# Accumulating DMAs in pieces of 8192 bytes, and a planner that runs GpSimd's and SyncE's transfers side by side

## The chip, the cores and the metric

The kernel runs on one core of one Trainium2 chip. The metric is the device time of one execution in microseconds (us). The engines are called TensorE (PE, with its weight loads PEld), VectorE (DVE), ScalarE (ACT), GpSimd (POOL) and SyncE (SP); each takes its instructions in order from a queue of its own. SyncE and GpSimd also issue DMAs, which run on the core's 16 DMA engines.

## The reference

One layer of a decoder trunk over 512 tokens of width 1024. A normed input is projected by one wide matrix; its columns feed four branches (forgetting attention A, an RG-LRU recurrence B, native sparse attention C, a spatial-gating MLP D). Each branch is gated and projected to 1024, the four are merged with sigmoid gates, and a last projection is added to the input.

```python
xn = rms_norm(x, norm_g)
z = xn @ w_in                      # 1024 x 10528
...
ys = jnp.stack([y_a * silu(ga), y_b * silu(gb), y_c * silu(gc), y_d * silu(gd)], axis=2)
proj = jnp.einsum('bsnw,nwd->bsnd', ys, w_branch)
merged = jnp.sum(jax.nn.sigmoid(mg.reshape(B, S, N_BRANCHES, D)) * proj, axis=2)
return x + merged @ w_out
```

All of it is float32.

## The kernel before

**Arithmetic.** Every float32 operand is split in a high part (a cast to fp32r) and a low part (the difference), and a product takes three matmuls of 128x512: high by high, low by high, high by low. For each weight tile of 128x1024 SyncE loads the raw 512 KB (`load`, tiles `r_...`, four buffers), GpSimd or ScalarE makes the high part (`hi_cast`), VectorE the low part (two subtractions, `wsplit`), and TensorE multiplies.

**Block sums.** The late projections (the gates mg0 to mg3, the branch projections wb1 and wb3, the output projection wo) are done with Strassen's scheme in Winograd's form: seven block products instead of eight, on sums and differences of weight blocks and of input blocks. The weight sums are formed in HBM by DMA alone: `sum_steps` lists for each family four base copies (`base`: s1, s3 from the weights, s2 from s1, 22 from s2) and four accumulating DMAs (`more`), which GpSimd issues and which add a block of 128 x 2048 floats (1 MB; for wb 128 x 1024 floats, 512 KB) to the copy in HBM. `x_sums` does the same with four sums of input blocks of 512 KB. A copy waits for the add whose result it reads, and an add for its base copy. The last argument of an accumulating DMA, `max_dma_last_dim`, is the largest piece in bytes in which a row is moved. The copies of mg0, mg2, mg1, wb1 and wb3 are issued by SyncE, those of mg3 and wo by GpSimd.

**Two ways of ordering.** Up to about 384 us (instructions that the profile puts on L231) all work is recorded first and then ordered by a planner, `Order`. From then on (L243) instructions stand in the order of the program text. The planner keeps a clock for each engine and a model of the shared things. `cost` gives each instruction a time to issue, a transfer time and, for DMAs, a delay until the data count as landed. `plan` then goes on engine by engine: whoever is free first takes, of the instructions whose needs are done at that time, the one that stands first in the program. The result is only an order for each engine's queue; at run time semaphores hold what isn't ready. So a cost in the planner moves no work by itself, but decides what stands behind what on each queue.

In the planner before, all DMAs share one wire: a transfer begins when the wire is free, at the earliest 1.3 us after its issue begins, takes size / 350e3 us from SyncE (size / 185e3 from GpSimd), and counts as done 0.86 us after its end; GpSimd's adds, and SyncE's DMAs into HBM tiles, count as done 10 us later still.

**Pace.** `tick` counts the steps of the dense matmul streams; every few steps (`BEAT`: 5 for the sums of this stretch) it records the next step of the sums, tied to the matmul just recorded. GpSimd's adds are moreover kept apart in the plan: each waits, in the plan alone, for the one before the last (`adds[-2]`).

**What GpSimd does besides.** In the planned stretch it makes most of the high parts of the weights, scales rows of the attention probabilities (p_a, p_s, p_w), fills operand tiles (`k_tiles` memsets kb_...; `spread` trs), copies key halves (`k_operand`, ka_...). After 384 us ScalarE takes over the casts of the block products, and GpSimd only paces (`paced_late`, tiles `mark`) and issues the late sums of mg3 and wo. The kernel is built with `dynamic_dma_scratch_size=1024`.

Of the kernel before, what the change touches and what calls it, by code (L numbers as in the profile page):

```python
# [14 lines left out]
ALU = mybir.AluOpType  # L15
AX = mybir.AxisListType
PSUM = bass.MemoryType.PSUM
# [50 lines left out]
class Order:  # L68
# [5 lines left out]
    def __init__(self, nc):  # L74
        self.eng = {"ACT": nc.scalar, "DVE": nc.vector, "POOL": nc.gpsimd, "PE": nc.tensor, "SP": nc.sync}
        self.on, self.ops, self.seen, self.ring, self.before, self.stacks = False, [], {}, {}, {}, {}
        self.free = dict.fromkeys(self.eng, 0.0)
        self.wire, self.shared, self.load, self.psum, self.bank = 0.0, (0.0, None), 0.0, set(), {}
        self.outside, self.floor, self.adds = set(), None, []
        self.end, self.pending, self.queued = {}, [], None  # L80

    def pool(self, real, stack, space):
# [48 lines left out]
    def cost(self, name, method, kw, aps):  # L131

        free = max(a.free_size() for _, a in aps)
        scalar = any(not w and x.free_size() == 1 for w, x in aps)
        wide = [x for w, x in aps if not w and x.free_size() > 1]
        if name == "PE":
            weights = kw["lhsT"] if "lhsT" in kw else wide[0]
            return aps[0][1].free_size() / 2400, 0.112 * max(64, min(128, weights.free_size())) / 128
        if method == "dma_start":
            size = 4  # L140
            for _, c in aps[0][1].ap:
                size *= c
            if name == "POOL":
                return 0.92, size / 185e3, 10.0
            return 0.37, size / 350e3, 10.0 if aps[0][1].tensor.name in self.outside else 0.0
        if name == "DVE":
            alone = bool(wide) and method not in ("tensor_reduce", "reciprocal", "memset") and not any(
                x.tensor.name in self.psum for x in wide)
            return 0.155 + free / 960 + 0.05 * scalar + 0.06 * (method == "tensor_tensor_scan" and free / 100), alone
        if name == "ACT":  # L150
            return 0.15 + free / 1140 + 0.09 * scalar + 0.15 * ("accum_out" in kw), False
        if method == "memset":
            return 0.1 + free / 1200, False
        return (0.09 + free / 540 if len(wide) > 1 and method == "tensor_tensor" else 0.18 + free / 1170), True
# [3 lines left out]
    def plan(self):  # L158

        ops, left, then, ready = self.ops, {}, {}, {}  # L160
        soon, able = {e: [] for e in self.eng}, {e: [] for e in self.eng}
        free, end, out = dict(self.free), self.end, []
        wire, shared, load, bank = self.wire, self.shared, self.load, dict(self.bank)
        margin = lambda e, m: self.WAKE[e] + (self.MARGIN[e] if ops[m][0] != e and ops[m][1] != "dma_start" else 0.0)
        for i in self.pending:
            name, need = ops[i][0], ops[i][4]
            for t in ops[i][6]:
                need.update((m, True) for m, *_ in self.seen.get(self.before.get(t), ()))
            ready[i], left[i] = 0.0, 0
            for m, whole in need.items():  # L170
                if m in end:
                    ready[i] = max(ready[i], end[m] + margin(name, m) if whole else 0.0)
                else:
                    left[i] += 1
                    then.setdefault(m, []).append(i)
            if not left[i]:
                heapq.heappush(soon[name], (ready[i], i))
        done, todo = {}, len(self.pending)
        while len(out) < todo:
            best = None  # L180
            for e in self.eng:
                t = free[e]
                while soon[e] and soon[e][0][0] <= t:
                    heapq.heappush(able[e], heapq.heappop(soon[e])[1])
                c = (t, e) if able[e] else (soon[e][0][0], e) if soon[e] else None
                best = min(best, c) if best and c else best or c
            t, e = best
            while soon[e] and soon[e][0][0] <= t:
                heapq.heappush(able[e], heapq.heappop(soon[e])[1])
            i = heapq.heappop(able[e])  # L190
            open_ = max((bank[x][1] + self.WAKE[e] for x in ops[i][7] if x in bank and bank[x][0] != e), default=0.0)
            if open_ > t:
                heapq.heappush(soon[e], (open_, i))
                continue
            a, b, *late = ops[i][5]
            if e == "PE":
                start = max(t + b, load)
                load, free[e], done[i] = start + a + 0.014, start + max(a - 0.098, 0.003), start + a + 0.172
            elif ops[i][1] == "dma_start":
                wire = max(wire, t + 1.3) + b  # L200
                free[e], done[i] = t + a, wire + 0.86 + sum(late)
            else:
                done[i] = t + a
                if b:
                    if shared[1] != e and shared[0] > t + 0.06:
                        done[i] = shared[0] - 0.06 + a
                    shared = done[i], e
                free[e] = done[i] - self.OVER[e]
            for x in ops[i][7]:
                bank[x] = e, done[i]  # L210
            out.append((i, dict(free), wire, shared, load, done[i]))
            for j in then.get(i, ()):
                f = ops[j][0]
                ready[j] = max(ready[j], done[i] + margin(f, i) if ops[j][4][i] else t)
                left[j] -= 1
                if not left[j]:
                    heapq.heappush(soon[f], (ready[j], j))
        return out
# [28 lines left out]
class _Pool:  # L247
    def __init__(self, order, real, space):
        self.order, self.real, self.names, self.lines = order, real, [], {}
        self.kind = {PSUM: order.psum, bass.MemoryType.DRAM: order.outside}.get(space, set())  # L250

    def tile(self, *args, tag=None, bufs=None, **kw):
        if tag is not None:
# [13 lines left out]
def tile_hybrid_layer(ctx: ExitStack, tc: tile.TileContext, x, xT, units, small, bsp, out):  # L267
    nc = tc.nc
    order = Order(nc)
    ACT, DVE, POOL, PE, DMA = (_Engine(order, e) for e in ("ACT", "DVE", "POOL", "PE", "SP"))  # L270
# [136 lines left out]
    def block(f, r, c):  # L407
        if f.startswith("wb"):
            return units[UIDX[f"{f}{c - 1}"], :, (r - 1) * 1024:r * 1024]
        return units[UIDX[f"{f}{c - 1}.{r - 1}"]]  # L410
# [3 lines left out]
    def sum_steps(f, copy):  # L414
        size = 1024 if f.startswith("wb") else 2048
        d = dsum[f] = {nm: dr.tile([P, size], F32, name=f"d{f}{nm}") for nm in ("s1", "s2", "22", "s3")}

        def base(nm, src):
            return lambda: copy.dma_start(d[nm], src)

        def more(nm, r, c):
            return lambda: POOL.dma_start(d[nm], block(f, r, c), accum_op=ALU.add, max_dma_last_dim=4096)

        return [base("s1", block(f, 1, 2)), base("s3", block(f, 1, 2)), more("s1", 1, 1), more("s3", 2, 2),
                base("s2", d["s1"]), more("s2", 2, 2), base("22", d["s2"]), more("22", 2, 1)]
# [180 lines left out]
    dxs = {nm: dr.tile([P, 1024], F32, name="dx" + nm) for nm in ("s1", "s2", "s3", "s4", "n11", "n21", "n22")}  # L606
# [8 lines left out]

    def x_sums():
        def more(nm, by):
            return lambda: POOL.dma_start(dxs[nm], dxs[by], accum_op=ALU.add, max_dma_last_dim=4096)

        return [more("s1", "n22"), more("s3", "n21"), lambda: DMA.dma_start(dxs["s2"], dxs["s1"]), more("s2", "n11"),  # L620
                more("s4", "s2")]
# [771 lines left out]
    late = ExitStack()  # L1393
# [535 lines left out]
```

## Time and profile before

| | |
|---|---|
| median of 3 runs | 703.0 us (702.05 to 704.62) |
| profiled execution | 705.58 us |
| its span, first to last instruction | 703.9 us |
| mean granted TensorE clock | 0.994 |
| DMA packets of SyncE's queue (q1) | 30208, 108.67 MB, 43.7% of 16 engines |
| DMA packets of GpSimd's queue (q0) | 7424, 35.65 MB, 24.7% of 16 engines |

A row of a group or of a timeline names the engine, the line of the code (a helper's line for nearly all instructions: L231 in the planned stretch, L243 behind it), the operation, and the tile written and those read; so instructions are found by their tiles. `dmg0s<-in_units_dram` is an add or a base copy for the sums of mg0, `dmg<-...` one for its tile 22, and `dwb1s`, `dmg3s`, `dwos`, `dxs` those of the others; POOLq marks a DMA that GpSimd issues, SPq one of SyncE. In a timeline what stands in brackets is how long the engine was idle before the row, and who ended that. A row of waits gives the engine and the tile that waited, who released it, and the us in total, the times and the longest. Durations of matmuls are longer than their share of the time, since matmuls overlap.

### The profile page before, as it was taken

What the parts mean: (1) busy time and instruction counts of PE and PEld (TensorE: products, weight loads), DVE (VectorE), ACT (ScalarE), POOL (GpSimd) and SP (SyncE); (2) the same over time, 40 slices, a digit from 0 to 9 for tenths busy, and PEclk for the clock granted to TensorE, in tenths of its full rate; (3) what the DMA queues carried; (4) which work ended last, traced back from release to release, by engine and by line L of the source; (5) the groups of instructions that cost most, each with busy time, mean ns of one, the idle gap of its engine ahead of it and who ended that gap; (6) DMA issues with size and microseconds to landing.
All of it is one profiled execution on the core that took longest, in us unless ns stands there. A gap on an engine that the chain in (4) does not pass through costs nothing.

```text
span 703.9 us, 9767 instructions
## 1 busy us (share of the span) xinstructions
PE 686.8 (98%) x3277; PEld 564.6 (80%) x3277; DVE 555.4 (79%) x1100; ACT 406.2 (58%) x766; POOL 202.5 (29%) x279
## 2 busy tenths in 40 slices
PE   8999999998979999999999999999999999999997
PEld 6888788887858888888777878888888888888886
DVE  6789778687576549898998669976888797948995
ACT  4563558575153127677656794445666666664861
POOL 4124864556173134445433122200110410100000
PEclk9999999999989999999999999999999999999999
DMA  8637078589789896976542224549899999997422
GB/s 312 247 119 240 25 215 270 152 203 247 162 248 311 223 237 192 202 153 185 106 87 78 88 85 155 168 142 383 250 313 310 301 328 327 314 307 259 142 90 90
DMA packets 38115, 145.44 MB, mean 207 GB/s; under 512 B 4129, under 2 KB 7585, under 8 KB 37665
## 3 DMA queue, kind: packets, MB, share of 16 engines
q1 hardware_dynamic: 30208, 108.67, 43.7%
q0 software_dynamic: 7424, 35.65, 24.7%
q8 instruction: 26, 0.43, 0.2%
q10 hardware_dynamic: 432, 0.49, 0.2%
q14 instruction: 25, 0.20, 0.1%
HBM read 139.56 MB, written 58.20 MB: 281 GB/s over the span
## 4 chain that ended last, share of the span: by engine, by line
PE 77%; DVE 9%; ACT 5%; issue 4%; POOL 2%; DMA 2%; SPq 0%; DVEq 0%; POOLq 0%; ACTq 0%
PE pj L243 4%; PE z_qc L231 3%; PE z_gd L231 3%; PE z_gb L243 3%; PE z_qa L231 3%; PE z_va L231 3%; PE tb L231 3%; PE z_ga L231 3%; PE outy L243 2%; PE mg0y L243 2%; PE mg3y L243 2%; PE mg1y L243 2%; PE mg2y L243 2%; PE z_ka L231 2%; PE o_s L231 2%
## 5 line engine op out<-in xcount | busy, mean ns | idle before, releaser
L243 DVE TENSOR_TENSOR w_mg<-r_mg,w_mg 128x512 fp32r<-128x512 f32 x48 | 31.9, 688 | 11.2 <-ACT w_mg L243 11.0
L243 PE MATMUL pj<-w_wb,yh 128*128 128x512 f32 x128 | 40.4, 390 | 0.0
L243 ACT CAST w_mg<-r_mg 128x1024 fp32r<-128x1024 f32 x24 | 25.2, 1049 | 10.3 <-issue 4.9
L243 POOL TENSOR_SCALAR mark<-mark 128x1 f32<-128x1 f32 x16 | 11.4, 711 | 66.6 <-ACT mark L243 66.5
L231 POOL TENSOR_SCALAR p_w<-p_w,nm_w 128x128 f32<-128x128 f32 (+3 forms) x32 | 18.1, 582 | 35.6 <-DVE nm_w L231 21.6
L243 PEld LDWEIGHTS pj<-w_wb,yh 128*128 128x128 f32 x128 | 24.0, 188 | 4.9
L231 POOL TENSOR_SCALAR p_s<-p_s,nm_s 128x128 f32<-128x128 f32 (+3 forms) x32 | 17.9, 593 | 28.3 <-DVE nm_s L231 19.4
L243 PE MATMUL pj<-w_wb,yl 128*128 128x512 f32 x64 | 25.4, 397 | 0.6 <-DVE yl L243 0.5
L231 ACT ACTIVATE p_w<-p_w,nm_w 128x256 f32<-128x256 f32 (+3 forms) x32 | 17.8, 555 | 13.9 <-DVE nm_w L231 12.3
L231 ACT CAST ph_a<-tb 128x512 fp32r<-128x512 f32 (+1 forms) x24 | 12.4, 518 | 20.2 <-PE tb L231 18.0
L231 PE MATMUL z_ga<-xh,w_ga 128*128 128x512 f32 x64 | 23.6, 426 | 0.4 <-DVE w_ga L231 0.4
L231 PE MATMUL z_xb<-xh,w_xb 128*128 128x512 f32 x64 | 23.2, 405 | 0.0
L231 PE MATMUL z_ud<-xh,w_ud 128*128 128x512 f32 x64 | 23.1, 411 | 0.0
L231 PE MATMUL z_gd<-xh,w_gd 128*128 128x512 f32 x64 | 22.7, 396 | 0.3 <-DVE sgd L231 0.3
L231 ACT ACTIVATE p_s<-p_s,nm_s 128x512 f32<-128x512 f32 (+3 forms) x32 | 17.9, 560 | 8.8 <-DVE nm_s L231 8.6
L231 ACT ACTIVATE p_a<-p_a,nm_a 128x512 f32<-128x512 f32 (+3 forms) x32 | 17.8, 558 | 8.2 <-DVE nm_a L231 8.1
L231 POOL TENSOR_SCALAR p_a<-p_a,nm_a 128x128 f32<-128x128 f32 (+3 forms) x32 | 18.6, 596 | 11.9 <-DVE nm_a L231 11.8
L243 DVE TENSOR_TENSOR w_wb<-r_wb,w_wb 128x512 fp32r<-128x512 f32 x28 | 18.3, 681 | 4.4 <-POOL w_wb L243 3.9
L243 PE MATMUL z_gb<-xh,w_gb 128*128 128x512 f32 x64 | 20.9, 390 | 0.0
L231 DVE CUSTOM_DVE_ANT_0 p_a<-s_a,maskm 128x512 f32<-128x512 f32 (+3 forms) x32 | 15.0, 486 | 5.6 <-PE tb L231 2.5
L231 DVE TENSOR_TENSOR pl_a<-tb,ph_a 128x512 fp32r<-128x512 f32 (+1 forms) x24 | 14.4, 598 | 4.7 <-ACT ph_a L231 4.5
L243 POOL TENSOR_SCALAR w_wb<-r_wb 128x1024 fp32r<-128x1024 f32 x8 | 10.1, 1264 | 26.9 <-PE pj L243 13.9
(744 smaller groups left out, 2419.4 us busy)
## 6 DMA issues: line engine op xcount, KB each, us to landing
r_mg<-in_units_dram SPq DMA_DIRECT2D x16, 512.0 KB, 6.9
r_wb<-in_units_dram SPq DMA_DIRECT2D x12, 512.0 KB, 5.0
dmg<-in_units_dram POOLq DMA_DIRECT2D x4, 1024.0 KB, 11.3
r_mg<-dmg SPq DMA_DIRECT2D x8, 512.0 KB, 9.0
dmg0s<-in_units_dram POOLq DMA_DIRECT2D x3, 1024.0 KB, 11.6
dmg2s<-in_units_dram POOLq DMA_DIRECT2D x3, 1024.0 KB, 11.3
dmg1s<-in_units_dram POOLq DMA_DIRECT2D x3, 1024.0 KB, 11.5
r_mg0s<-dmg0s SPq DMA_DIRECT2D x6, 512.0 KB, 4.7
```

Source lines behind the costliest of these rows:

```text
L231: getattr(self.eng[name], method)(*args, **kw)
L243: return lambda *args, **kw: real(*args, **kw).ins
```

## The change

Two things are changed. The accumulating DMAs of `sum_steps` and `x_sums` are cut in pieces of at most 8192 bytes instead of 4096. And the planner models two lanes of transfers: SyncE's, and GpSimd's adds. An add begins 1.7 us after its issue begins (or when the add before it is through), takes size / 155e3 us and 0.3 of the time it shares with a transfer of SyncE's, and counts as done 2.2 + 5 us later. A transfer of SyncE's runs at 0.33 of its rate while an add is on the way. Copies from HBM to HBM take size / 233e3 us, and what goes to an HBM tile counts as done 3 us later instead of 10. A new set `inner` holds the names of the SBUF tiles, by which the planner tells a copy from a store.

```diff
-        self.wire, self.shared, self.load, self.psum, self.bank = 0.0, (0.0, None), 0.0, set(), {}
-        self.outside, self.floor, self.adds = set(), None, []
+        self.wire, self.shared, self.load, self.psum, self.bank = (0.0, 0.0), (0.0, None), 0.0, set(), {}
+        self.inner, self.outside, self.floor, self.adds = set(), set(), None, []
...
             if name == "POOL":
-                return 0.92, size / 185e3, 10.0
-            return 0.37, size / 350e3, 10.0 if aps[0][1].tensor.name in self.outside else 0.0
+                return 0.92, size / 155e3, 5.0
+            inside, known = (aps[j][1].tensor.name in self.outside for j in (0, 1)), aps[1][1].tensor.name in self.inner
+            copy, source = inside
+            if copy and (source or not known):
+                return 0.37, size / 233e3, 3.0
+            return 0.37, size / 350e3, 3.0 if copy else 0.0
...
-        wire, shared, load, bank = self.wire, self.shared, self.load, dict(self.bank)
+        wire, added, shared, load, bank = *self.wire, self.shared, self.load, dict(self.bank)
...
             elif ops[i][1] == "dma_start":
-                wire = max(wire, t + 1.3) + b
-                free[e], done[i] = t + a, wire + 0.86 + sum(late)
+                free[e] = t + a
+                if e == "POOL":
+                    start = max(t + 1.7, added)
+                    added = start + b + 0.3 * min(b, max(0.0, wire - start))
+                    done[i] = added + 2.2 + late[0]
+                else:
+                    start = max(t + 1.3, wire)
+                    held = 0.33 * max(0.0, added - start)
+                    wire = start + b / 0.33 if held >= b else max(start, added) + b - held
+                    done[i] = wire + 0.86 + late[0]
...
-            out.append((i, dict(free), wire, shared, load, done[i]))
+            out.append((i, dict(free), (wire, added), shared, load, done[i]))
...
-        self.kind = {PSUM: order.psum, bass.MemoryType.DRAM: order.outside}.get(space, set())
+        self.kind = {PSUM: order.psum, bass.MemoryType.DRAM: order.outside}.get(space, order.inner)
...
-            return lambda: POOL.dma_start(d[nm], block(f, r, c), accum_op=ALU.add, max_dma_last_dim=4096)
+            return lambda: POOL.dma_start(d[nm], block(f, r, c), accum_op=ALU.add, max_dma_last_dim=8192)
...
-            return lambda: POOL.dma_start(dxs[nm], dxs[by], accum_op=ALU.add, max_dma_last_dim=4096)
+            return lambda: POOL.dma_start(dxs[nm], dxs[by], accum_op=ALU.add, max_dma_last_dim=8192)
```

## The prediction

> **What bounds the kernel now.** I read the page's busy shares first, then what TensorE (PE) waited for between 60 and 384 us, where the order is the planner's (ten rows, longest first; the six left out are at most 0.5 us each), then one row per stretch.
>
> ```profile
> span 703.9 us, 9767 instructions
> PE 686.8 (98%) x3277; PEld 564.6 (80%) x3277; DVE 555.4 (79%) x1100; ACT 406.2 (58%) x766; POOL 202.5 (29%) x279
> ```
> ```profile
> PE s_s L231 <- DVE q_c L231: 4.1, 1, 4.1
> PE o_a L231 <- DVE pl_a L231: 1.8, 1, 1.8
> PE s_w L231 <- DVE q_c L231: 1.2, 1, 1.2
> PE tb L231 <- DVE sc L231: 0.5, 1, 0.5
> ```
> ```profile
> core 0: us, PE busy (x) PEld busy (x) DVE busy (x) ACT busy (x) POOL busy (x), PEclk, DMA share, GB/s
> 158.00:174.00 16.00, 14.20 (x75) 11.20 (x74) 12.60 (x19) 8.06 (x19) 10.80 (x14) 1.00 0.98 282
> ...
> 199.50:204.00 4.50, 0.40 (x2) 0.01 (x1) 4.42 (x6) 2.74 (x4) 4.34 (x4) 1.00 0.94 192
> 204.00:212.00 8.00, 7.54 (x21) 5.36 (x22) 7.97 (x11) 2.41 (x3) 3.57 (x5) 0.57 0.75 175
> ...
> 440.00:640.00 200.00, 200.00 (x906) 166.44 (x905) 159.82 (x262) 118.89 (x168) 24.79 (x31) 1.00 0.89 289
> ```
>
> PE is the bound: 98% busy. So the change can win only what PE loses, and its largest loss is one place: 4.1 us without work near 200 us, and right behind it a granted clock of 0.57 over 8 us, which costs 8 x (1 - 0.57) = 3.4 us more. Together 7.5 us. The 1.8 us wait (it lies in 158 to 174) left the clock at 1.00. From 440 to 640 us PE is busy for all 200 us: nothing can be won there.
>
> Who made PE wait? The chain of waits from 174 to 205 us says it (a merged row's first number is its start, the second its length):
>
> ```profile
> 175.34 1.05 POOL w_vd.11_966 L231
> 176.38 9.26 issue
> ...
> 186.26 1.37 POOL w_ga L231
> 187.63 6.73 issue
> 194.36 0.91 POOL dmg2s L231
> ...
> 197.56 0.52 POOL kb_c L231
> ...
> 200.34 1.34 DVE trs L231
> ...
> 203.13 0.76 DVE q_c L231
> 203.88 0.14 issue
> 204.02 0.78 PE s_s L231 x2
> ```
>
> GpSimd (POOL) stood still twice, 9.26 + 6.73 = 16.0 us, each time just ahead of an accumulating DMA. Behind it on its in-order queue stood the cast of w_ga, the memsets of kb_c and of trs; VectorE waited for these, and PE for VectorE's q_c. "issue" means that no semaphore in the profile explains the stand. GpSimd's own timeline, and the landing of each of its DMAs (view of DMA issues, cut to the 1 us around each issue; last number is us from issue to landing), do:
>
> ```profile
> 174.05 0.93 POOL L231 DMA_DIRECT2D dmg2s<-in_units_dram  x1 [2.68 <-PE tb L231]
> 185.66 0.89 POOL L231 DMA_DIRECT2D dmg0s<-in_units_dram  x1 [9.28 <-issue]
> 194.36 0.91 POOL L231 DMA_DIRECT2D dmg2s<-in_units_dram  x1 [6.73 <-issue]
> 254.59 0.87 POOL L231 DMA_DIRECT2D dmg1s<-in_units_dram  x1
> 263.96 0.83 POOL L231 DMA_DIRECT2D dwb3s<-in_units_dram  x1
> ```
> ```profile
> dmg2s<-in_units_dram POOLq DMA_DIRECT2D x1, 1024.0 KB, 11.3
> ...
> dmg0s<-in_units_dram POOLq DMA_DIRECT2D x1, 1024.0 KB, 8.4
> ...
> dmg1s<-in_units_dram POOLq DMA_DIRECT2D x1, 1024.0 KB, 12.4
> ```
>
> 174.05 + 11.3 = 185.35, and the next add goes at 185.66. 185.66 + 8.4 = 194.06, and the next goes at 194.36. Twice an add of 1 MB is let go 0.3 us after the one before it has landed. But the 512 KB add of 263.96 went while the 1 MB add of 254.59 was still under way (254.59 + 12.4 = 267.0). A 1 MB add is 128 rows of 8192 bytes, now cut in 256 pieces; a 512 KB add has 128 pieces of 4096. So 256 + 128 pieces fit into whatever GpSimd's queue has room for, and 256 + 256 don't.
>
> **The change, part by part.**
>
> *Pieces of 8192 bytes.* A 1 MB add becomes 128 pieces; a 512 KB add keeps its 128, for its rows are 4096 bytes. 128 + 128 is less than the 256 + 128 that fit, and a third still fits. What goes is the stand ahead of the adds. What is late next at 200 us? ScalarE's q_c:
>
> ```profile
> 199.24 1.38 ACT L231 ACTIVATE q_c<-qt_c,cc 64x512 fp32r<-64x512 f32 x2 [0.44 <-PE qt_c L231]
> ```
>
> It ends at 200.62; VectorE's last q_c step (0.76) would then end near 201.4, and PE go on near 201.5 instead of 204.0. So at least 2.5 us of the wait go, leaving about 1.6, less than the wait of 1.8 that left the clock alone; at most all 4.1 go. Gain: 2.5 + 3.4 = 5.9 to 4.1 + 3.4 = 7.5. I take 3.7 + 3.4 = 7.1, near the upper end: the typical wait in the planner's stretch is a few tenths, once the engines come when the plan has them come. The issue itself gets shorter by about 0.1 us (0.89 for 256 pieces, 0.83 for 128) for each of 20 adds: 2 us of GpSimd, which is 29% busy; worth nothing by itself.
>
> [...]
>
> *The planner's costs.* They move no work by themselves; they change the order in which all five engines get their instructions up to about 384 us. In its terms a 1 MB add goes from 1.3 + 5.7 + 0.86 + 10 = 17.8 us to 1.7 + 6.8 + 2.2 + 5 = 15.7 (landings above: 8.4 to 12.4), a 1 MB copy from 1.3 + 3.0 + 0.86 + 10 = 15.2 to 1.3 + 4.5 + 0.86 + 3 = 9.7, and a 512 KB load beside an add from 1.5 us of wire to as much as 4.5.
>
> ```profile
> r_ud<-in_units_dram SPq DMA_DIRECT2D x4, 512.0 KB, 7.2
> ...
> dmg1s<-in_units_dram SPq DMA_DIRECT2D x2, 9.9
> ```
>
> The copies' 9.9 agree with the new 9.7, so adds are put closer behind their base copies, with next to no margin: if one lands late, GpSimd waits for it, and the casts behind it too. The trace shows no such order, so I bound it: the waits other than the 4.1 are at most 1.8 + 1.2 + 7 x 0.5 = 6.5 us. Drawn anew they could vanish (6.5 won) or double (6.5 lost). I take 0: the costs come closer to the landings, which speaks for fewer waits, but any new order brings some of its own.
>
> *Bigger pieces on shared engines.* Loads beside adds may come later. The cover: the first r_ud load is issued at 236.94, and PE uses w_ud at 253.66:
>
> ```profile
> 187.67 1.29 DVE L231 TENSOR_TENSOR w_ga<-r_ga,w_ga 128x512 fp32r<-128x512 f32 x2 [5.34 <-POOL w_ga L231]
> ...
> 236.94 11.79 SPq L231 DMA_DIRECT2D r_ud<-in_units_dram  x4
> ...
> 247.63 1.66 POOL L231 TENSOR_SCALAR w_ud<-r_ud 128x1024 fp32r<-128x1024 f32 x1
> ...
> 253.66 0.48 PE L231 MATMUL z_ud<-xh,w_ud 128*128 128x512 f32 x1
> ```
>
> 16.7 us, less 7.2 landing, 1.7 cast and 1.3 for the low part (a row of the same step for w_ga), leaves 6.4 us to spare. I cost it at nothing while loads come less than 6.4 us later; beyond that each us is PE's. [...]
>
> *The late sums (wo, mg3)* change in piece size alone. GpSimd stands there too, once for 13.2 us, and PE in those 200 us loses nothing:
>
> ```profile
> POOL dwos L243 <- issue: 13.2, 1, 13.2
> ```
>
> **Sum.** -7.1 + 0 + 0 = -7.1 us. The profiled execution took 705.6 us (span 703.9 and 1.7 around it) and would take 698.5; it lies 2.6 above the median of the three runs shown, and I carry the difference over: 703.0 - 7.1 = 695.9. With its bounds (-7.5 - 6.5 and -5.9 + 6.5) this case spans 689.0 to 703.6.
>
> **The rivals.**
>
> *Nothing is lifted.* The stand is not about the number of pieces; GpSimd still waits for each add before the next. [...] Against it: the 128-piece add that went 3 us before the 256-piece one had landed. Time 703, moved only by the new order.
>
> *Lifted, but given back.* The new order puts waits of 3.6 to 6.5 us where there were none. For it: margins are cut while copies of 9.9 us meet a plan of 9.7. Against it: GpSimd's many short waits cost PE nothing today. Time about 701 (703.0 - 7.1 + 5.1, the middle of these).
>
> *Slower: SyncE held by an add.* SyncE waits in order for an add to land before the base copy that reads it, and the weight loads stand behind it:
>
> ```profile
> SPq L231 <- DMA dmg1s<-in_units_dram: 12.4, 1, 12.4
> ```
>
> That was the longest, and it cost nothing where it fell. With GpSimd free two adds are queued at once, and the second lands one add later: 12.4 + 8.4 = 20.8 us. In front of the r_ud loads (236 us) with 6.4 us to spare PE would wait 14.4 and pay 3.4 for the clock: 703.0 - 7.1 + 17.8 = 713.7. It decides the sign from a hold of 6.4 + (7.1 - 3.4) = 10.1 us on, and is measurable from 13.6. Against it: the planner knows SyncE's order, and now counts loads beside adds as slow.
>
> **How the numbers follow.** This kernel's measurement can tell about 0.5%, 3.5 us, from no change. Forecast 0.62 (695.9; below 699.5 while less than 3.6 of the 7.1 us is given back). Lifted but given back 0.14 and nothing lifted 0.09: both within 0.5%. SyncE held 0.15: slower. So faster 0.62, within 0.5% 0.23, slower 0.15. The range takes in the forecast's bounds and the two cases near 701 to 703, and leaves out the slower one: 689.5 to 704.0.
>
> **What would show it.** Right: the 1 MB adds as 128 packets of 8192 bytes; GpSimd's "issue" stands ahead of them gone before 384 us; adds issued while the one before is under way; no PE wait above 2 us and no slice of the clock under 1.00 near 200 us. Wrong: a stand still ending 0.3 us after a landing (nothing lifted); GpSimd waiting for a base copy, or SyncE for an add, with a PE wait behind it (given back, or slower). A second clock drop anywhere would make the prediction wrong by itself.

## The result, and the profile after

The changed kernel takes 699.47 us (median of 5 runs, 699.12 to 700.01), the kernel before 703.85 beside it (5 runs, 702.05 to 704.84): ratio 0.994, 95% interval 0.9923 to 0.9958. That is 4.4 us, or 0.6%. The forecast was 7.1 us. The two profiled executions differ by more, 705.58 against 699.47 us, their spans 703.9 against 697.7: runs of the kernel before with a mean clock of 0.999 took 701.6 to 703.5 us, those with 0.991 or 0.992 705.5 to 707.8, and the profiled one, with 0.994, lies 1.7 above the median, while of the changed kernel the run with a clock of 1.000 (699.12) is hardly shorter than the profiled one with 0.996 (699.47). A line that was L231 is L243 now, and L243 is L255.

The page of the changed kernel: span, clock and DMA queues (packets, MB, share of 16 engines):

```profile
span 697.7 us, 9760 instructions
...
PE 685.3 (98%) x3277; PEld 564.4 (81%) x3277; DVE 555.9 (80%) x1100; ACT 406.2 (58%) x766; POOL 208.9 (30%) x279
...
PEclk9999999999999999999999999999999999999999
...
q0 software_dynamic: 4608, 35.65, 23.7%
```

GpSimd's queue went from 7424 packets to 4608 with the same bytes. 20 adds of 1 MB save 128 packets each, 2560; the 256 that are left are the four 512 KB sums of input blocks, in 64 pieces each instead of 128. PE is still busy 98% of the time, so the gain must lie in its gaps. GpSimd's adds, from its timeline, with their landings (DMA issues cut to 1 or 1.5 us around each):

```profile
134.92 0.80 POOL L243 DMA_DIRECT2D dmg0s<-in_units_dram  x1
135.47 1.13 POOL L243 DMA_DIRECT2D dmg2s<-in_units_dram  x1
...
171.88 0.83 POOL L243 DMA_DIRECT2D dmg0s<-in_units_dram  x1
174.85 0.84 POOL L243 DMA_DIRECT2D dmg2s<-in_units_dram  x1
```
```profile
dmg0s<-in_units_dram POOLq DMA_DIRECT2D x1, 1024.0 KB, 10.0
...
dmg2s<-in_units_dram POOLq DMA_DIRECT2D x1, 1024.0 KB, 14.4
...
dmg0s<-in_units_dram POOLq DMA_DIRECT2D x1, 1024.0 KB, 7.7
...
dmg2s<-in_units_dram POOLq DMA_DIRECT2D x1, 1024.0 KB, 13.2
```

The second add now goes 0.55 us behind the first, and at 174.85 while the add of 171.88 has 4.7 us to go. The stands of 9.3 and 6.7 us are gone. (One stand of 5.6 us that the profile also puts down to "issue" is there now, but ahead of a cast of w_ga at 181.33, not of an add; e1_pieces below has it too.) PE's waits from 60 to 384 us (the longest four), then SyncE's:

```profile
PE z_ga L243 <- DVE w_ga L243: 2.1, 1, 2.1
PE tb L243 <- DVE pl_w L243: 0.6, 2, 0.4
PE z_gd L243 <- DVE sgd L243: 0.6, 1, 0.6
PE z_kv L243 <- DVE v_a L243: 0.5, 1, 0.5
```
```profile
SPq L243 <- DMA dmg0s<-in_units_dram: 24.1, 1, 24.1
```

The 4.1 us for q_c are gone, and 2.1 us for w_ga stand in their place (before, PE waited 0.4 us for w_ga). Where the time came from is read from the same four stretches in both traces, before and then after:

```profile
core 0: us, PE busy (x) PEld busy (x) DVE busy (x) ACT busy (x) POOL busy (x), PEclk, DMA share, GB/s
158.00:174.00 16.00, 14.20 (x75) 11.20 (x74) 12.60 (x19) 8.06 (x19) 10.80 (x14) 1.00 0.98 282
196.00:208.00 12.00, 7.44 (x32) 5.17 (x31) 9.17 (x11) 7.06 (x11) 9.05 (x13) 0.86 0.89 218
208.00:216.00 8.00, 8.00 (x30) 6.47 (x30) 6.16 (x10) 1.69 (x4) 3.23 (x4) 0.79 0.96 303
300.00:384.00 84.00, 82.11 (x460) 68.30 (x459) 77.05 (x204) 56.70 (x147) 35.90 (x57) 1.00 0.50 119
```
```profile
158.00:174.00 16.00, 15.54 (x83) 12.60 (x82) 12.96 (x22) 9.60 (x22) 12.28 (x16) 1.00 0.78 218
196.00:208.00 12.00, 9.89 (x41) 7.49 (x40) 10.62 (x15) 6.55 (x9) 7.27 (x7) 0.86 0.92 256
208.00:216.00 8.00, 8.00 (x40) 6.76 (x39) 6.32 (x19) 4.43 (x15) 2.40 (x5) 1.00 0.94 358
300.00:384.00 84.00, 83.01 (x452) 68.45 (x451) 76.94 (x199) 57.41 (x142) 31.83 (x49) 1.00 0.27 70
```

PE's idle time is a stretch's length less its first busy time; what the clock costs is estimated as the length times (1 - PEclk). From 196 to 216 us PE was idle 4.6 us and lost 12 x 0.14 + 8 x 0.21 = 3.4 to the clock; now 2.1 and 1.7. That is 4.1 us. From 158 to 174 us 1.3 us came, from 300 to 384 us 0.9: together 6.3 us, as much as the difference of the spans (6.2); no other stretch differs by more than 0.3 us.

### The profile page after: what moved, and what is told of

The parts are those of the page before. It is cut to its first block, busy times and chain, and to the rows that moved or that the text cites. A ratio compares the mean times of both kernels' runs of the same rounds, so it can differ in the third digit from the quotient of the medians.

```text
span 697.7 us, 9760 instructions
## 1 busy us (share of the span) xinstructions
PE 685.3 (98%) x3277; PEld 564.4 (81%) x3277; DVE 555.9 (80%) x1100; ACT 406.2 (58%) x766; POOL 208.9 (30%) x279
## 3 DMA queue, kind: packets, MB, share of 16 engines
q0 software_dynamic: 4608, 35.65, 23.7%
## 4 chain that ended last, share of the span: by engine, by line
PE 82%; DVE 10%; ACT 4%; issue 2%; DMA 1%; POOL 0%; SPq 0%; DVEq 0%; ACTq 0%; POOLq 0%
PE pj L255 4%; PE z_ga L243 3%; PE z_qc L243 3%; PE z_gd L243 3%; PE z_vd L243 3%; PE z_gb L255 3%; PE z_qa L243 3%; PE tb L243 3%; PE z_va L243 3%; PE outy L255 3%; PE mg0y L255 2%; PE mg3y L255 2%; PE mg1y L255 2%; PE mg2y L255 2%; PE z_ka L243 2%; PE z_ud L243 2%
## 5 line engine op out<-in xcount | busy, mean ns | idle before, releaser
L255 POOL TENSOR_SCALAR mark<-mark 128x1 f32<-128x1 f32 x16 | 17.4, 1089 | 103.6 <-ACT mark L255 103.5
L255 DVE TENSOR_TENSOR w_mg<-r_mg,w_mg 128x512 fp32r<-128x512 f32 x48 | 31.8, 688 | 11.1 <-ACT w_mg L255 11.0
L255 PE MATMUL pj<-w_wb,yh 128*128 128x512 f32 x128 | 40.6, 390 | 0.0
L255 ACT CAST w_mg<-r_mg 128x1024 fp32r<-128x1024 f32 x24 | 25.2, 1050 | 10.3 <-issue 4.9
L243 POOL TENSOR_SCALAR p_w<-p_w,nm_w 128x128 f32<-128x128 f32 (+3 forms) x32 | 18.1, 582 | 36.1 <-DVE nm_w L243 26.4
L255 PEld LDWEIGHTS pj<-w_wb,yh 128*128 128x128 f32 x128 | 24.0, 188 | 4.9
L243 POOL TENSOR_SCALAR p_s<-p_s,nm_s 128x128 f32<-128x128 f32 (+3 forms) x32 | 18.3, 597 | 29.7 <-DVE nm_s L243 25.2
L255 PE MATMUL pj<-w_wb,yl 128*128 128x512 f32 x64 | 25.4, 396 | 0.6 <-DVE yl L255 0.6
L243 PE MATMUL z_ga<-xh,w_ga 128*128 128x512 f32 x64 | 23.3, 416 | 2.1 <-DVE w_ga L243 2.1
L243 ACT CAST ph_a<-tb 128x512 fp32r<-128x512 f32 (+1 forms) x24 | 12.4, 517 | 20.0 <-PE tb L243 19.9
L243 PE MATMUL z_xb<-xh,w_xb 128*128 128x512 f32 x64 | 23.8, 408 | 0.0
L243 PE MATMUL z_ud<-xh,w_ud 128*128 128x512 f32 x64 | 23.4, 406 | 0.0
L243 PE MATMUL z_gd<-xh,w_gd 128*128 128x512 f32 x64 | 22.7, 398 | 0.6 <-DVE sgd L243 0.6
L243 ACT ACTIVATE p_s<-p_s,nm_s 128x512 f32<-128x512 f32 (+3 forms) x32 | 17.9, 560 | 8.2 <-DVE nm_s L243 7.9
L243 ACT ACTIVATE p_a<-p_a,nm_a 128x512 f32<-128x512 f32 (+3 forms) x32 | 17.8, 558 | 7.2 <-DVE nm_a L243 7.1
L255 DVE TENSOR_TENSOR w_wb<-r_wb,w_wb 128x512 fp32r<-128x512 f32 x28 | 18.3, 681 | 4.3 <-POOL w_wb L255 3.8
L243 POOL TENSOR_SCALAR p_a<-p_a,nm_a 128x128 f32<-128x128 f32 (+3 forms) x32 | 18.1, 581 | 11.9 <-DVE nm_a L243 11.7
L243 ACT ACTIVATE p_w<-p_w,nm_w 128x256 f32<-128x256 f32 (+3 forms) x32 | 17.8, 556 | 6.4 <-DVE nm_w L243 6.3
L255 PE MATMUL z_gb<-xh,w_gb 128*128 128x512 f32 x64 | 20.9, 390 | 0.0
L243 DVE CUSTOM_DVE_ANT_0 p_a<-s_a,maskm 128x512 f32<-128x512 f32 (+3 forms) x32 | 14.9, 485 | 4.6 <-PE s_a L243 2.0
L255 POOL TENSOR_SCALAR w_wb<-r_wb 128x1024 fp32r<-128x1024 f32 x8 | 10.3, 1293 | 26.4 <-PE pj L255 13.9
L243 DVE TENSOR_TENSOR pl_a<-tb,ph_a 128x512 fp32r<-128x512 f32 (+1 forms) x24 | 14.3, 598 | 4.3 <-ACT ph_a L243 4.1
```

Of the source, the lines that this page charges most:

```text
L243: getattr(self.eng[name], method)(*args, **kw)
L255: return lambda *args, **kw: real(*args, **kw).ins
```

## The experiments

Each run has the kernel before beside it; ratios are to that.

**Which half of the change?** The pieces alone (`e1_pieces`: the kernel before with the two 4096 made 8192, its planner and all its orders kept) and the planner alone (`e2_plan`).

```diff
 e2_plan, on the changed kernel, in sum_steps and x_sums
-... accum_op=ALU.add, max_dma_last_dim=8192)
+... accum_op=ALU.add, max_dma_last_dim=4096)
```

> The kernel before with pieces of 8192 bytes alone: the planner and every queue's order stay as before. Theory (room: GpSimd stands because 256 + 256 pieces don't fit its queue): the stands of 9.3 and 6.7 us ahead of adds go, PE's wait of 4.1 us near 200 us goes or falls under 2, the clock stays at 1.00, and the time falls by 5.9 to 7.5 us, to 696 to 698. Rival (order: the gain came from the new order): the stands may go, but the time stays within 1.5 us of 703.9.

> The changed kernel with pieces of 4096 bytes again: the new order alone. Theory (room): adds that the new order issues close together stand again until 0.3 us after the landing of the one before (the pair at 135 us, 0.5 us apart, by about 8 us; the pair at 172 and 175 us by about 6); 702 to 708. Rival (order): no slower than the changed kernel, 699 to 701.

e1_pieces: 699.67 us (698.55 to 701.5), ratio 0.9947 (0.9926 to 0.9969). e2_plan: 707.86 (706.88 to 708.37), ratio 1.0055 (1.0036 to 1.0074). The pieces alone give the gain, as far as the intervals can tell; the new order alone costs 0.55%, and beside the larger pieces it is worth nothing that can be told. But e1_pieces misses the 696 to 698 that was expected of it. Its PE waits (first the longest), and three of the stretches above, are:

```profile
PE s_s L231 <- DVE q_c L231: 1.6, 1, 1.6
PE z_ga L231 <- DVE w_ga L231: 1.3, 1, 1.3
PE s_w L231 <- DVE q_c L231: 1.1, 1, 1.1
```
```profile
158.00:174.00 16.00, 16.00 (x89) 13.59 (x87) 12.80 (x23) 9.88 (x21) 12.81 (x16) 1.00 1.03 290
196.00:208.00 12.00, 8.96 (x31) 6.26 (x30) 11.46 (x15) 5.53 (x8) 6.14 (x8) 0.72 0.41 131
300.00:384.00 84.00, 82.03 (x450) 67.61 (x450) 77.54 (x202) 57.78 (x144) 32.99 (x52) 1.00 0.49 119
```

GpSimd's stands ahead of these adds are gone, with the order of the kernel before, and the 1.6 us for q_c is the most that the prediction left of the 4.1. But a wait for w_ga follows (the 1.1 us for s_w come later, near 335 us), PE is idle for 3.0 us from 196 to 208 us, and the clock costs 12 x 0.28 = 3.4, as much as before: in this trace (701.50 us, 1.8 above the median) the place gives only 1.5 us, and 158 to 174 us another 1.8. In e2_plan GpSimd stands again, for 9.8 us ahead of a 1 MB add at 145.25 and here, in its timeline:

```profile
256.64 0.83 POOL L243 DMA_DIRECT2D dwb1s<-in_units_dram  x1
257.18 1.21 POOL L243 DMA_DIRECT2D dmg1s<-in_units_dram  x1
...
269.89 0.81 POOL L243 DMA_DIRECT2D dwb3s<-in_units_dram  x1 [5.08 <-issue]
```
```profile
dwb1s<-in_units_dram POOLq DMA_DIRECT2D x1, 512.0 KB, 12.9
```

Adds of 128 and 256 pieces go half a microsecond apart; the third, of 128, is let go 0.35 us after the first has landed (256.64 + 12.9 = 269.54). So 384 pieces fit and 512 don't. The new order puts adds closer behind each other, which costs where the room is too small for two: behind the stand of 9.8 us, PE waits for a key copy (ka_a) of GpSimd's that stood there.

```profile
PE s_a L243 <- POOL ka_a L243: 4.5, 1, 4.5
```

**Is it the room?** The changed kernel with `dynamic_dma_scratch_size` at 512 instead of 1024.

```diff
-    nc = _bacc.Bacc("TRN2", ..., dynamic_dma_scratch_size=1024)
+    nc = _bacc.Bacc("TRN2", ..., dynamic_dma_scratch_size=512)
```

> The changed kernel with dynamic_dma_scratch_size 512 instead of 1024: same order, same pieces, half of what the kernel reserves for GpSimd's DMAs. Theory (room): 128 + 128 pieces no longer fit, so the stands come back, each ending about 0.3 us after the landing of the add before; 702 to 708, as with 4096-byte pieces. Rival (landing: what ended the stands was the bigger piece itself, not room): no stands, 699 to 700.

730.62 us (728.48 to 731.27), ratio 1.0371 (1.0341 to 1.0402). GpSimd's timeline, and the landing of the first add:

```profile
134.47 0.81 POOL L243 DMA_DIRECT2D dmg0s<-in_units_dram  x1
144.81 0.84 POOL L243 DMA_DIRECT2D dmg2s<-in_units_dram  x1 [9.52 <-issue]
```
```profile
dmg0s<-in_units_dram POOLq DMA_DIRECT2D x1, 1024.0 KB, 10.0
```

134.47 + 10.0 = 144.47, and the next add goes 0.34 us later: now two adds of 128 pieces don't fit. Up to 384 us GpSimd stands three times more ahead of an add (8.6, 6.3 and 7.5 us), and the first two of these end 0.3 us after the landing of the add before (223.99 + 11.7 and 279.22 + 7.9, the next adds at 235.97 and 287.39). The stands follow the room, and the room this size: two adds of 128 pieces were under way together with 1024 (134.92 and 135.47 above), and with 512 the second stands. That is the cause of the stands; how much of the size a piece takes was not shown. The cost was far above what was expected, for PE then waits 9.1, 6.0, 4.3 and 2.7 us at four places, and the mean clock is 0.981 instead of 0.996.

**What is left near 199 us?** 2.1 us of wait and 1.7 of clock. First, SyncE's hold of 24.1 us: it stands ahead of the loads of w_ga. With the planner's delay of an add back at 10 us SyncE's order changes and its longest stand on an add is 14.3 us.

```diff
-                return 0.92, size / 155e3, 5.0
+                return 0.92, size / 155e3, 10.0
```

> The changed kernel, but the planner counts an add as landed 10 us after its transfer instead of 5. In the order that it makes SyncE's copy of mg0's tile 22, which waits for an add, stands behind four weight loads instead of ahead of them. Theory (the 2.1 us that PE still waits for w_ga at 199 us, and the 1.7 us of clock behind it, come from SyncE being held 24.1 us by that copy): both go, 699.5 - 3.8 = 695.7, within 694.5 to 697. Rival (w_ga is late because VectorE and ScalarE are in arrears there whatever SyncE does): the wait stays at 1.5 us or more and the time within 1 us of 699.5.

699.35 us (699.18 to 699.59), ratio 0.9937 (0.9915 to 0.996): the same. PE waits 2.5 us at the same place, this time with ScalarE's cast of w_ga named. The hold isn't the cause: the rival's wait and time came. VectorE's timeline of the changed kernel shows what stands there:

```profile
193.98 1.03 DVE L243 TENSOR_TENSOR trs<-t2v,cc 128x496 f32<-128x496 f32 x1 [3.38 <-ACT t2v L243]
...
197.51 1.22 DVE L243 TENSOR_TENSOR tblv<-trs,tblv 128x1024 fp32r<-128x1024 f32 x1 [1.24 <-POOL tblv L243]
198.66 1.51 DVE L243 SCALAR_TENSOR_TENSOR kb_c<-kt_s,cc,ka_c 64x512 fp32r<-64x512 f32 x2
200.19 2.46 DVE L243 TENSOR_TENSOR w_ga<-r_ga,w_ga 128x512 fp32r<-128x512 f32 x2
202.68 1.53 DVE L243 SCALAR_TENSOR_TENSOR q_c<-qt_c,cc,q_c 64x512 fp32r<-64x512 f32 x2
```

VectorE stands idle for 3.4 us, and from 197.5 on has 6.7 us of work in a row, with both things PE needs at its end. Every third high part is ScalarE's (`hi_cast`), so this one, while GpSimd is idle from 186.4 to 196.4. Three kernels gave both of ScalarE's casts of w_ga to GpSimd and let the planner draw the rest anew (e5 on the changed kernel, e6 on e4_add10, e7 on e1_pieces).

```diff
-        hi_cast(w[:, 0, :], raw)
+        hi_cast(w[:, 0, :], raw, key[:2] != "ga")
```

> The changed kernel, but the high parts of the weight tiles w_ga (the gate of branch A, one stretch of the planner's program near 190 to 225 us) are all made by GpSimd; in the changed kernel one of them is ScalarE's, and stands in its queue behind four evictions, four copies and q_c. My theory of what is left of the loss near 199 us: PE's 2.1 us wait for w_ga and the 1.7 us that the clock costs behind it come from that one cast on ScalarE's queue, while GpSimd stands idle for 10 us just before. Then the wait and the half clock go, and the time is 699.5 - 2.1 - 1.7 = 695.7. Rival 1: the planner puts this weight tile late whoever casts it (its record of work begins anew there, and the engines' queues behind it are full), so the wait of about 2 us stays under another name: 699.5 within 1. Rival 2: the cast on GpSimd takes 1.66 us instead of ScalarE's shorter one and holds back the copies of keys behind it: 700 to 702.

> As e5_after_pool (all casts of w_ga on GpSimd), with the planner's delay after an add at 10 us instead of 5, so that SyncE no longer stands 24 us behind one add and this cast stands earlier in GpSimd's queue. Theory (ScalarE's queue makes w_ga late): 695.7, and if SyncE's hold had a share of it that e4_add10 alone could not show, up to 0.5 less. Rival 1 (late whoever casts it): 699.4 within 1, with PE's wait near 199 us still above 1.5 us. Rival 2 (GpSimd's longer cast holds back others): 700 to 702.

> The kernel before with pieces of 8192 bytes alone (the planner's costs as before, so nearly the order of e1_pieces), and all casts of w_ga on GpSimd. e1_pieces took 699.7, with PE waits of 1.6, 1.3 and 1.1 us near 200 us and two slices of half clock. Theory (ScalarE's queue makes w_ga late): the 1.3 us wait for w_ga goes and, as the waits there then come to less than 3 us together, half of the clock's loss too: 699.7 - 1.3 - 1.7 = 696.7. Rival (late whoever casts it): 699.7 within 1. If the memsets and key copies on GpSimd come later behind the extra cast: 700 to 702.

| | us (lowest to highest) | ratio (95%) |
|---|---|---|
| e5_after_pool | 704.13 (698.09 to 706.98) | 0.9982 (0.9952 to 1.0013) |
| e6_add10_pool | 708.96 (704.6 to 710.7) | 1.0056 (1.0028 to 1.0084) |
| e7_pieces_pool | 702.74 (700.77 to 704.34) | 0.9982 (0.9968 to 0.9996) |

All three miss. In e5 the wait for w_ga is gone, and 2.6 us for q_c stand there: the two have changed places in VectorE's queue. Its profiled execution took 698.73 us, and what its longer runs lose no trace shows. In e7 a wait of 3.6 us for nm_w comes up elsewhere. In e6 the place itself is nearly mended, but the new order loses more behind it:

```profile
196.00:208.00 12.00, 10.55 (x50) 8.08 (x48) 11.47 (x13) 4.31 (x7) 10.06 (x11) 1.00 0.37 122
216.00:240.00 24.00, 19.84 (x81) 15.53 (x80) 13.69 (x33) 4.61 (x13) 7.28 (x9) 0.86 0.93 239
240.00:300.00 60.00, 56.47 (x294) 47.44 (x293) 37.01 (x102) 29.02 (x75) 20.84 (x28) 0.97 0.66 175
```

24 - 19.84 + 60 - 56.47 = 7.7 us of idle PE, and 24 x 0.14 + 60 x 0.03 = 5.2 for the clock; e4_add10 was idle for 1.1 us from 216 to 300, at full clock. Such an edit changes the whole plan behind it, so it can't test one cast. The next four keep the plan: all instructions are ordered as before, and only then one cast is moved, of the second w_ga tile. In e11 it goes to GpSimd at its old place; in e8 (on e4_add10), e9 (on the changed kernel) and e10 (on e1_pieces) its cast and its subtractions go ahead of trs, into the idle time.

```diff
 settle(), behind the plan; "mine" are the cast and the two subtractions of w_ga01, "at" VectorE's first step on t2v
+            out = [o for o in out if o not in mine]
+            k = out.index(at[0])
+            out = out[:k] + mine + out[k:]
...
+            if name == "ACT" and any(x.startswith("w_ga01") for x in self.ops[i][6]):
+                self.eng["POOL"].tensor_scalar(*args, 1.0, 0.0, op0=ALU.mult, op1=ALU.add)
+                continue
```

> The kernel of e4_add10 with one weight tile made earlier and nothing else reordered: the planner runs as before, and then the high part of the second w_ga tile goes to GpSimd behind tblk (at 186 us, where GpSimd stands idle for 9.4 us) instead of ScalarE's queue at 198.8, and its two subtractions go to VectorE ahead of trs (where VectorE stands idle for 4.3 us) instead of 199.9. The runs with all casts of w_ga on GpSimd let the planner redraw everything behind, and so said little. My theory of the residue now: VectorE is in arrears from 197.5 us on, and w_ga and q_c, for which PE waits, stand in that queue behind kb_c and trs. Taken out of the arrears, w_ga costs PE nothing and q_c comes 2.2 us earlier: 699.35 - 2.5 (the wait) - 1.7 (the half clock behind it) = 695.2. Rival: the loss is bound elsewhere (PE then waits as long for q_c, kt_w or the next weight tile): a wait above 1.5 us stays between 195 and 210 us, and the time is 698.5 to 700.

> The same edit on the changed kernel (planner's delay 5). There SyncE's hold of 24.1 us lets the raw w_ga tile land only near 193 us, so GpSimd's early cast would wait for it until then, and VectorE's trs behind the subtractions would start about 1.4 us later than its 194.0. If VectorE's arrears are the cause: the wait of 2.1 us and the half clock go, 699.47 - 2.1 - 1.7 = 695.7. If SyncE's hold has a price that the arrears have hidden so far, it shows here and not in e8_add10_early: 697 to 699, with PE waiting for trs's followers (kb_c, q_c).

> The same edit on e1_pieces (pieces of 8192 bytes, the planner's costs as before). There PE waits 1.6 us for q_c and 1.3 for w_ga, with two slices of half clock. The edit can take the 1.3 us and, if less than 2 us of waits stays together, one half-clock stretch: 699.7 - 1.3 - 1.7 = 696.7. With the clock as it was: 698.4. Rival (loss bound elsewhere): 699.7 within 1.

> The kernel of e4_add10 in which that one cast goes to GpSimd at the place where the planner had it on ScalarE (behind ka_c, ahead of tblv), with all other queues as they were. If ScalarE's queue were the cause, the 2.5 us wait would go: 695.2. By VectorE's arrears the cast is ready near 198.2 instead of 199.9, but the subtractions still stand behind trs until 198.9: the wait shrinks by 1.0 us to 1.5 us, and the time is 698.3, or 696.6 if the clock stays whole after the shorter wait.

| | us (lowest to highest) | ratio (95%) | mean clock of the profiled run |
|---|---|---|---|
| e8_add10_early | 696.89 (696.07 to 697.11) | 0.9899 (0.988 to 0.9919) | 1.000 |
| e9_after_early | 697.3 (697.06 to 697.89) | 0.991 (0.9893 to 0.9927) | 0.999 |
| e10_pieces_early | 697.07 (696.28 to 698.89) | 0.9908 (0.989 to 0.9927) | 0.996 |
| e11_add10_moved | 696.93 (696.76 to 697.09) | 0.9903 (0.9886 to 0.992) | 0.999 |

One cast was worth 2.2 to 2.6 us: the intervals of e8 and e11 lie below that of the changed kernel. They touch that of e4_add10, on which the two are built, but none of their runs (at most 697.11 us) comes near its fastest (699.18). (Line numbers are shifted by the edit.) In e11 the wait of 2.5 us becomes two of 0.8 (for GpSimd's cast) and 0.7 (for VectorE's low part), as PE's timeline shows:

```profile
197.97 0.50 PE L246 MATMUL z_ga<-xh,w_ga 128*128 128x512 f32 x1 [0.77 <-POOL w_ga L244]
...
199.36 0.73 PE L246 MATMUL z_ga<-xh,w_ga 128*128 128x512 f32 x2 [0.65 <-DVE w_ga L246]
```

2.46 - 1.42 = 1.0 us, and 1.7 for the clock, which stays whole: 2.7, the difference of the spans (697.9 and 695.2). That is the theory of VectorE's arrears with its clock (expected 696.6); ScalarE's queue as sole cause (695.2) falls. In e4_add10 both queues held w_ga back, ScalarE's by the 1.0 us; in the changed kernel ScalarE's cast ended at 198.40, and VectorE came to w_ga only at 200.19. In e8 no wait is left before 204 us, and VectorE's w_ga takes 1.29 us:

```profile
189.88 1.29 DVE L252 TENSOR_TENSOR w_ga<-r_ga,w_ga 128x512 fp32r<-128x512 f32 x2
193.28 1.03 DVE L252 TENSOR_TENSOR trs<-t2v,cc 128x496 f32<-128x496 f32 x1 [2.10 <-ACT t2v L252]
```

It misses 695.2 by 1.7; a new wait of 1.4 us (for nm_s) comes behind it. e8 is no faster than e11, so moving the subtractions as well gave nothing that can be told. In e9, with SyncE's hold in place, GpSimd waits 5.6 us for the raw tile. The time lies in the 697 to 699 that was put down to a price of the hold, but PE's waits for trs's followers, the sign of it, don't come (0.2 us for kb_c), and the time is only 0.4 us above e8's; the orders differ in more than the hold, so 0.4 is a bound by one comparison. In e10 the wait for w_ga is gone, and in its trace (698.89 us, 1.8 above the median) the waits for q_c (1.6 us, and 1.1 near 332) and half of the clock's loss (8 x 0.21 = 1.7 us, at 0.79 from 200 to 208 us) stay, as expected.

## Why the prediction was right or wrong

**The bound and the cause: right.** PE lost its time near 200 us, GpSimd stood for want of room for pieces, 384 fit and 512 don't, and 128-piece adds don't stand with a `dynamic_dma_scratch_size` of 1024, not even a third beside two (the changed kernel, 257.32): e1_pieces takes the stands away with the orders kept, e3_ring512 brings them back.

**"A 512 KB add keeps its 128": right for wb, wrong for the input sums** (64 each). It changed nothing, since it makes room. Two small sums are off as well, and nothing hangs on them: 16.7 - 7.2 - 1.7 - 1.3 is 6.5 and not 6.4, and the range begins at 689.5, above the 689.0 that it was to take in.

**The first rival, "nothing is lifted": wrong.** In the changed kernel the add of 135.47 goes while that of 134.92, which lands after 10.0 us, is under way, and in e1_pieces the stands of 9.3 and 6.7 us are gone with every order kept.

**"I take 3.7 + 3.4 = 7.1, near the upper end": this step failed.** I reasoned that "the typical wait in the planner's stretch is a few tenths, once the engines come when the plan has them come". The place gave 2.4 + 1.7 = 4.1 us: 1.3 less of the wait and 1.7 less of the clock, together the missing 3.0. The question what is late next was asked for ScalarE's q_c alone; VectorE's queue, where w_ga and q_c stand in a row, wasn't read. In the trace the 2.1 us of wait that remained had a stretch of lower clock behind them (0.50 from 202 to 204 us), 1.7 us in all. That a whole clock alone would bring these 1.7 us back isn't shown: the run of the changed kernel with a clock of 1.000 was only 0.35 us shorter than the profiled one.

**The new order "taken at 0": right beside 8192-byte pieces, but it is a cost without them.** Alone it costs 0.55% (e2_plan), inside the bound of 6.5 us. The whole change gave 1.3 us at 158 to 174 us (before, the wait of 1.8 for pl_a) and 0.9 from 300 on (the 1.2 of s_w for q_c) that I had not counted. e1_pieces has no idle PE from 158 to 174 either (16.00 busy of 16), so that part belongs to the pieces, and the later one, which e1_pieces doesn't have (82.03 of 84) and e2_plan does (83.12), to the order.

**"I carry the difference over": wrong by 1.7 us.** Between the profiled executions the gain was 6.1 us, not 7.1; between the medians it was 4.4. The profiled execution of before lies 1.7 above its median now, that of after on its own. The clocks of the runs of before (0.991 to 0.999) say that the 3.4 us aren't lost in every one of them, so part of their gain isn't in the medians.

**Loads beside adds at nothing: right.** r_ud lands after 9.3 us instead of 7.2, 2.1 of 6.4 us of cover. That isn't the pieces: with them alone it is 7.1, with the order alone 9.8.

**The slower rival: its hold came, its price didn't.** SyncE stood 24.1 us, more than the 20.8 worked out, but ahead of the w_ga loads, where the buffer and VectorE's queue hid it: nothing that can be told in e4_add10, no more than 0.4 us in e9. The rival "given back" describes the residue better than I had it: a wait of 2.1 us where there were 0.4.

**The signs.** Packets, stands and overlapping adds came as named. "No PE wait above 2 us" and "no slice of the clock under 1.00" failed, and they were right to be named: both are the missing 3 us. The chance of 0.62 was on a gain above 3.5 us, and 4.4 is little above it; as 2.2 us of the 6.3 between the traces came from places that I hadn't counted, that it came out so is in part luck.

## What to carry to other kernels

Where an in-order engine stands ahead of a DMA with no semaphore to blame, compare its release with the landing of an earlier DMA and count pieces in flight: larger pieces were worth more here than another order (ratios 0.9947 and 1.0055, each alone), and that order without the room cost time. When a stand is lifted, read the queue of each engine behind it for what is late next, and take as gain only what is left when the longest of these stays. Test one instruction with the order of the others kept; an edit ahead of a planner tests the planner's luck, 12 us apart here (e6, where a second cast moves too, and e11).

## What the runs showed of the hardware

- Short waits of PE and the clock behind them: waits of 2.1 us (the changed kernel) and 2.5 us (e4_add10) each had 1.7 us of lost clock behind them, 4.1 us (before) had 3.4. Waits of 0.8 + 0.7 (e11_add10_moved) and of 1.4 us (e8_add10_early) left it whole, 1.8 us (before, at 158 to 174) did too, and 1.6 us had 1.7 behind them in e10_pieces_early and nothing, with 0.8 more beside them, in e7_pieces_pool (1.00 from 196 to 216 us). So the length alone doesn't decide between 1.4 and 2.1 us, and what does is open; runs of one kernel differ too (the changed kernel's clocks are 0.996 to 1.000). The 3 us in e7_pieces_pool's expectation and the 2 us in e10_pieces_early's were estimates from e1_pieces (3.0 us idle, 3.4 of lost clock), the changed kernel (2.1 and 1.7) and before (1.8 and none); as limits no run shows them.
- What GpSimd's DMAs in flight have room for: with a `dynamic_dma_scratch_size` of 1024, adds of 128 + 256 pieces were under way together and 256 + 256 weren't (stands of 9.3 and 6.7 us in before, 9.8 in e2_plan), and three of 128 were, once (the changed kernel, from 257.32 us); with 512, 128 + 128 weren't (stands of 9.5 and 6.3 us in e3_ring512). Ahead of an add without room GpSimd stood up to 13.2 us (before, at 576.85), until 0.3 us after a landing.
- Halving `dynamic_dma_scratch_size` from 1024 to 512 cost 31 us in this kernel (730.62 us in e3_ring512 against 699.47).
- The same two subtractions on VectorE took 1.29 us where GpSimd was idle (e8_add10_early, at 189.88) and 2.46 us (the changed kernel, at 200.19) while GpSimd worked on ka_c, w_ga and w_w1k.
